# Reading the moving operand of every wide float32r product from two places in turn

## The chip, the cores and the metric

The kernel runs on one core of one Trainium2 chip. The metric is the device time of one execution in microseconds (us); lower is better. Engines are named as the profile names them: PE (the matmul array) with PEld (its weight loads), DVE, ACT, POOL, SP (which issues most DMAs).

## The reference

Two layers on 512 tokens of width 1024, all in float32. Each layer is a mixer and a SwiGLU feed-forward part, with norms, shifts, scales and gates that come from a conditioning vector.

```python
for layer in range(DEPTH):                       # DEPTH = 2
    mod = (cond @ ada_w[layer] + ada_b[layer])[:, None, :]
    sh1, sc1, g1, sh2, sc2, g2 = jnp.split(mod, 6, axis=-1)
    u = rms_norm(h, norm_g[layer, 0]) * (1.0 + sc1) + sh1
    y = hgrn2_mixer(...) if layer == 0 else dilated_attention_mixer(...)
    h = h + (1.0 + g1) * rms_norm(y, norm_g[layer, 1])
    u = rms_norm(h, norm_g[layer, 2]) * (1.0 + sc2) + sh2
    gate, up = jnp.split(u @ ffn_w_in, 2, axis=-1)
    y = (jax.nn.silu(gate) * up) @ ffn_w_out       # D_FF = 2816
    h = h + (1.0 + g2) * rms_norm(y, norm_g[layer, 3])
```

`hgrn2_mixer` projects u to queries, forget gates, values and output gates, and runs a chunked linear recurrence. `dilated_attention_mixer` projects u to queries, keys and values of three groups (dilations 1, 4, 16), applies rotary positions, and merges the groups' attention by their log-sums. Almost all arithmetic is in the dense projections.

## The kernel before, in words

**Products.** PE multiplies a stationary block of 128x128 by a moving block of 128 rows and up to 512 columns, into PSUM. To keep float32 accuracy, both factors are split into a high part (rounded to the type float32r) and a low rest: `oh`/`ol`, `hi`/`lo`, `uh`/`ul`, `th`/`tl`. ACT writes the high part by a copy with a cast, DVE the rest by a subtraction. Each product is three matmuls, high by high, high by low and low by high (helper `three`, L583 to L586; `run` at L965 and `products` at L1986 do the same). Each matmul has its own weight load. "Wide" is a float32r matmul with 256 or 512 moving columns.

**Stages, in order of time** (us from the start of the span):

- to 80: conditioning, and the token-major value product of layer 0 (`v_pass`, L1321: 8 weight rows x 3 parts x 8 banks = 192 matmuls of 512 columns).
- 80 to 280: the HGRN projections (`block`: 24 blocks x 24 = 576 matmuls of 512 columns), with the recurrence of eight heads (DVE mostly, and small matmuls) between them, and conditioning work of later parts.
- 280 to 360: the mixer's output product, the norm, and the first four column blocks of the feed-forward input (`mixer_out`, `half`, `block`).
- 360 to 525: the other 18 column blocks in `seven_products` (Strassen's scheme with seven half-size products: 84 matmuls of 256 columns a block; L965).
- 525 to 640: the feed-forward output (`prods` in `ffn`: 22 row blocks x 4 token blocks x 2 halves x 3 = 528 matmuls of 512 columns). Before each row block ACT and DVE split the middle activations (`part`: L580, L581) and the weights (L90, L91).
- 640 to 720: norms, the attention's value products (`v_prod`, `tok_proj`).
- 720 to 1140: attention. Here a planner (`Plan`) keeps a list of tasks with costs in us, due times and dependencies, tries several rules, and writes out the order for all engines. Its products are of three kinds: query and key blocks of group 0 (`plain`: 8 heads x 2 x 24 = 384 matmuls of 512 columns), of the other groups by seven products (`sevens`: 16 x 84 = 1344 of 256 columns), and values by seven products (`value_unit`: 4 x 7 x 24 = 672 of 256 columns).
- 1140 to 1487: output product, norm and feed-forward part of layer 1, as in layer 0.

In each of the two output products (mixers) there are 192 matmuls of 512 columns and then, in the first feed-forward blocks, 192 of 256 columns (`half`, L832, L835) and 96 of 512; `v_prod` and `tok_proj` have 96 of 512 each.

**Order.** In `mixer_out`, `seven_products`, the ends of `ffn` and the start, the order is written by hand (`manual_schedule`); elsewhere a scheduler of the framework orders the instructions; in attention `Plan` does.

**Places.** Tiles have offsets of 16 or 48 columns (`R0`, `V0`) and pads, so that operands stand at chosen addresses. `seven_products` and `products` also issue three extra matmuls ("asides") at the start of some runs of 256-wide products, with a moving operand shifted by 16 columns; their result is overwritten by the product that follows:

```python
if i == 0:
    for _ in range(3):
        pe.matmul(s.both, R[0][:, 0:P], uh[:, 0, 16:272], start=True, stop=True, ...)   # L992 to L994
```

The moving operand of a wide matmul is a row of neighbouring columns, its output a row of neighbouring columns of a PSUM bank.

Of the kernel before, what the change touches and what calls it, by code (L numbers as in the profile page):

```python
# [17 lines left out]
P = 128  # L18
# [16 lines left out]
WHOLE = ("quarters", "half")  # L35

# [104 lines left out]
class Plan:  # L141
# [5 lines left out]
    def __init__(self):  # L147
        self.tasks, self.names, self.seq, self.asides = [], {}, {}, set()
# [88 lines left out]
    def run(self):  # L237
# [15 lines left out]
        narrow = []  # L253
        for t in [t for t in done if t["eng"] == "PE"] + [{}]:
            if t.get("narrow"):
                narrow.append(t)
                continue
            first = next((k for k, u in enumerate(narrow) if u["aside"]), len(narrow))
            if len(narrow) - first >= 12:
                self.asides.add(narrow[first]["id"])  # L260
            narrow = []
# [40 lines left out]
def block_kernel(tc, x, c, positions, ada_w, ada_b, norm_g, hgrn_w_in, lower, hgrn_norm_g, hgrn_w_out,  # L302
# [8 lines left out]
    with ExitStack() as ctx:  # L311
# [271 lines left out]
        def three(ps, ah, al, bh, bl, start, stop, part=False):  # L583
            pe.matmul(ps, ah, bh, start=start, stop=False, skip_group_check=part)  # L584
            pe.matmul(ps, ah, bl, start=False, stop=False, skip_group_check=part)  # L585
            pe.matmul(ps, al, bh, start=False, stop=stop, skip_group_check=part)  # L586
# [18 lines left out]
        class Turn:  # L605
# [100 lines left out]
        def mixer_out(oT, otp, gate, l, side, close, made=None):  # L706
# [122 lines left out]
            for kt in range(KT):  # L829
                a = kt * 256  # L830
                for m, w in enumerate(fw[0]):
                    pe.matmul(pss[0][:, tok], w[:, a:a + P], uh[:, kt, tok], start=kt + m == 0, stop=False)  # L832
            for kt in range(KT):
                a = kt * 256
                pe.matmul(pss[0][:, tok], fw[0][0][:, a:a + P], ul[:, kt, tok], start=False, stop=kt == KT - 1)  # L835
# [53 lines left out]
        def seven_products(fs, mid, seeded, spare, th, tl):  # L889
# [71 lines left out]
            def run(ps, w, o, us, begin):  # L961
                for kt in range(4):
                    a = slice(o + kt * P, o + (kt + 1) * P)
                    for m, (x, y) in enumerate(((0, 0), (0, 1), (1, 0))):
                        pe.matmul(ps, w[x][:, a], us[kt][y], start=begin and kt + m == 0, stop=kt == 3 and m == 2,  # L965
# [10 lines left out]
            with tc.manual_schedule(engines=ORDERED):  # L976
# [10 lines left out]
                for i in range(len(fs)):  # L987
# [329 lines left out]
        def v_pass(e, which, hf, t):  # L1317
# [3 lines left out]
            pe.matmul(vbanks[hf, t], a, w, start=e == 0 and which == 0, stop=e == KT - 1 and which == 2)  # L1321
# [23 lines left out]
        with tc.manual_schedule(engines=ORDERED):  # L1345
# [121 lines left out]
            for (hf, t), b in vbanks.items():  # L1467
                (act.copy if hf == 0 else dve.tensor_copy)(v_tok[:, t, hf * 512:(hf + 1) * 512], b)
# [132 lines left out]
        def gate_pair(p):  # L1601
            whi, wlo = st.take()
            for k in range(2):
                ps = block(whi, wlo, k * P, 256)
                sg = fresh(qp, [P, S], "Q", 2)
                act.activation(sg, ps, AF.Sigmoid)
                dve.tensor_mul(sg, sg, ps)
# [917 lines left out]
```

## Time and profile before

| what | value |
|---|---|
| runs | 1492.56, 1493.22, 1494.55 us; median 1493.22 |
| span of the profiled execution | 1492.8 us, 25296 instructions |
| last matmul starts | 1486.3 us |
| PE busy | 1468.0 us (98%), 9915 matmul records |
| DVE, ACT, POOL busy | 74%, 54%, 13% |
| granted clock of PE | 0.999 of full speed, mean |

The profiled execution is known by its span: 1492.8 us, 0.4 us under the median of the runs. The "busy" time of a matmul is modelled and longer than its share of a stream (matmuls overlap), so the pace of a stream is read from the starts of neighbouring rows, not from durations. Durations on ACT and DVE are of one instruction. "x36" is a count; a line such as L585 can be that of a helper.

### The profile page before, as it was taken

Reading aid. Unit: us, or ns where it says so; the run is one execution under the profiler, and the core shown is the slowest. Engines: PE = TensorE matmul, PEld = TensorE weight load, DVE = VectorE, ACT = ScalarE, POOL = GpSimd, SP = SyncE. Lnnn points to the kernel's source line nnn. Section 1 sums busy time; section 2 is a strip of 40 time slices with the busy share of each in tenths; the row PEclk is TensorE's granted clock in tenths of the full one; section 3 lists DMA queues with packets and bytes.
Section 4 is the critical chain, followed back from the end, with each engine's and each line's share of the span. In section 5 each row is a group of like instructions: output and inputs, shape, how many; then the busy total and the mean of one; then the engine's idle time right before and its main releaser. Section 6 shows DMA issues by size and latency. Waiting matters only on the chain. (4 is left out here: it accounts for less than half of the span.)

```text
span 1492.8 us, 25296 instructions
## 1 busy us (share of the span) xinstructions
PE 1468.0 (98%) x9915; PEld 1318.0 (88%) x9915; DVE 1102.1 (74%) x1800; ACT 799.7 (54%) x1484; POOL 191.0 (13%) x173
## 2 busy tenths in 40 slices
PE   8999999999999999999999999999999999999998
PEld 6777788888999988778999999998988899999886
DVE  4578589488888875777798877888776978887533
ACT  4433433374555542257647878567885555555231
POOL 1011002030111100131001010001012211110100
PEclk9999999999999999999999999999999999999999
DMA  9556454213343346544334443354352333434531
GB/s 309 176 182 210 153 187 142 85 57 85 114 114 114 114 158 215 198 141 141 106 117 131 133 121 93 82 167 119 91 194 89 107 92 114 113 114 143 196 113 57
DMA packets 212872, 201.10 MB, mean 135 GB/s; under 512 B 8920, under 2 KB 170640, under 8 KB 212496
## 3 DMA queue, kind: packets, MB, share of 16 engines
q1 hardware_dynamic: 209776, 192.71, 41.6%
q10 hardware_dynamic: 1952, 6.65, 1.2%
q8 instruction: 78, 1.28, 0.4%
q0 software_dynamic: 1024, 0.12, 0.2%
q14 instruction: 42, 0.34, 0.1%
HBM read 192.30 MB, written 5.30 MB: 132 GB/s over the span
## 5 line engine op out<-in xcount | busy, mean ns | idle before, releaser
L90 ACT CAST hi<-raw 128x2048 fp32r<-128x2048 f32 x41 | 78.3, 1910 | 129.4 <-DMA raw<-in_ffn_w_out_dram 78.2
L1986 PE MATMUL ps_mm<-apart,hiq 128*128 128x256 f32 (+1 forms) x608 | 142.3, 326 | 0.8 <-ACT xs L2101 0.7
L91 DVE TENSOR_TENSOR lo<-raw,hi 128x2048 fp32r<-128x2048 f32 x41 | 97.9, 2391 | 57.8 <-ACT hi L90 57.7
L584 PE MATMUL ps_mm<-uh,hi 128*128 128x512 f32 (+1 forms) x368 | 133.8, 364 | 0.0
L585 PE MATMUL ps_mm<-ul,hi 128*128 128x512 f32 (+1 forms) x368 | 131.2, 356 | 1.1 <-DVE ul L684 1.1
L586 PE MATMUL ps_mm<-uh,lo 128*128 128x512 f32 (+1 forms) x368 | 131.3, 357 | 0.0
L1986 PEld LDWEIGHTS ps_mm<-apart,hiq 128*128 128x128 f32 x608 | 99.9, 189 | 9.4 <-ACT xs L2101 1.2
L956 DVE TENSOR_TENSOR loq<-raw,hiq 128x1024 fp32r<-128x1024 f32 x72 | 84.9, 1221 | 22.6 <-ACT hiq L952 22.6
L965 PE MATMUL ps_mm<-th,hiq 128*128 128x256 f32 x360 | 99.4, 276 | 0.0
L965 PE MATMUL ps_mm<-tl,hiq 128*128 128x256 f32 x360 | 99.4, 276 | 0.0
L965 PE MATMUL ps_mm<-th,loq 128*128 128x256 f32 x360 | 99.4, 276 | 0.0
L1986 PE MATMUL ps_mm<-apart,loq 128*128 128x256 f32 (+1 forms) x304 | 97.4, 320 | 0.5 <-DVE loq L2123 0.5
L936 POOL TENSOR_TENSOR raw<-raw 128x512 f32<-128x512 f32 x36 | 48.4, 1344 | 327.4 <-DVE spare L932 170.6
L585 PE MATMUL ps_mm<-lo,oh 128*128 128x512 f32 x208 | 81.6, 392 | 4.4 <-DVE lo L91 4.4
L584 PEld LDWEIGHTS ps_mm<-uh,hi 128*128 128x128 f32 x368 | 69.2, 188 | 15.4 <-issue 6.1
L952 ACT CAST hiq<-raw 128x1024 fp32r<-128x1024 f32 x72 | 72.1, 1047 | 19.4 <-DVE raw L940 16.1
L584 PE MATMUL ps_mm<-hi,oh 128*128 128x512 f32 x208 | 81.5, 393 | 0.1
L585 PEld LDWEIGHTS ps_mm<-ul,hi 128*128 128x128 f32 x368 | 69.3, 188 | 11.8 <-DVE ul L684 1.5
L586 PEld LDWEIGHTS ps_mm<-uh,lo 128*128 128x128 f32 x368 | 69.1, 188 | 10.4
L1986 PE MATMUL ps_mm<-uh,hiq 128*128 128x256 f32 x256 | 71.8, 281 | 0.0
L1986 PE MATMUL ps_mm<-ul,hiq 128*128 128x256 f32 x256 | 71.2, 278 | 0.0
L1986 PE MATMUL ps_mm<-uh,loq 128*128 128x256 f32 x256 | 71.2, 278 | 0.0
(484 smaller groups left out, 4688.6 us busy)
## 6 DMA issues: line engine op xcount, KB each, us to landing
raw<-in_ada_w_dram SPq DMA_DIRECT2D x40, 1024.0 KB, 5.2
raw<-in_ffn_w_in_dram SPq DMA_DIRECT2D x144, 256.0 KB, 4.1
raw<-in_ffn_w_out_dram SPq DMA_DIRECT2D x22, 1024.0 KB, 4.9
raw<-in_attn_w_in_dram SPq DMA_DIRECT2D x64, 256.0 KB, 4.2
raw<-in_hgrn_w_in_dram SPq DMA_DIRECT2D x12, 1024.0 KB, 5.4
raw<-in_attn_w_in_dram SPq DMA_DIRECT2D x12, 1024.0 KB, 5.3
raw<-in_ffn_w_in_dram SPq DMA_DIRECT2D x8, 1024.0 KB, 5.2
raw<-in_attn_w_in_dram SPq DMA_DIRECT2D x16, 512.0 KB, 5.3
```

Of the source, the lines that this page charges most:

```text
L90: self.nc.scalar.copy(hi, t)
L91: self.nc.vector.tensor_sub(lo, t, hi.bitcast(F32))
L584: pe.matmul(ps, ah, bh, start=start, stop=False, skip_group_check=part)
L585: pe.matmul(ps, ah, bl, start=False, stop=False, skip_group_check=part)
L586: pe.matmul(ps, al, bh, start=False, stop=stop, skip_group_check=part)
L936: pool.tensor_add(r[:, 2], r[:, 2], r[:, 0])
L952: act.copy(hi, src)
L956: dve.tensor_sub(lo, src, hi.bitcast(F32))
L965: pe.matmul(ps, w[x][:, a], us[kt][y], start=begin and kt + m == 0, stop=kt == 3 and m == 2, skip_group_check=True)
L1986: pe.matmul(dst(), x, y, start=begin and i == 0, stop=i == len(todo) - 1, skip_group_check=True)
```

## The change

Four views are added. `TAKE` reads a moving operand in blocks of 256 columns, and in each block column n and column n+128 in turn: 0, 128, 1, 129 and so on. `LAID` writes the output as before to neighbouring PSUM columns (it only has the same shape as `TAKE`). So output columns stand in the order in which they were read. `SEEN` reads such a row in the right order, with a step of two columns, and `PLACED` is the plain row that it is put in. All wide float32r products take `TAKE` and `LAID`.

The columns come back in order at the first reader that needs it: copies, gates, additions out of PSUM, or the split of `mid` in `part`. In `value_unit` the weights are instead split in such an order (`SEEN2`, `PLACED2` in `cut`) that the product comes out in order. Sums of squares and elementwise work between rows in the same order stay as they were.

The asides are gone with the code that placed them, and the planner's costs of products are other numbers. Eleven functions that nothing called (`qk_evac` to `pv_n`) are gone too.

```diff
+TAKE = lambda t: t.rearrange("p (x a n) -> p x n a", a=2, n=P)
+LAID = lambda t: t.rearrange("p (x n a) -> p x n a", a=2, n=P)
+SEEN = lambda t: t.rearrange("p (x n a) -> p x a n", a=2, n=P)
+PLACED = lambda t: t.rearrange("p (x a n) -> p x a n", a=2, n=P)
+SEEN2 = lambda t: t.rearrange("p s (n a) -> p s a n", a=2)
+PLACED2 = lambda t: t.rearrange("p s (a n) -> p s a n", a=2)
...
         def three(ps, ah, al, bh, bl, start, stop, part=False):
+            ps, bh, bl = LAID(ps), TAKE(bh), TAKE(bl)
             pe.matmul(ps, ah, bh, start=start, stop=False, skip_group_check=part)
...
-                dve.tensor_mul(self.yg[t, k], self.y[k][t], self.gate[:, k * 512:(k + 1) * 512])
+                dve.tensor_mul(PLACED(self.yg[t, k]), SEEN(self.y[k][t]), PLACED(self.gate[:, k * 512:(k + 1) * 512]))
...
-                        pe.matmul(ps, w[x][:, a], us[kt][y], start=begin and kt + m == 0, stop=kt == 3 and m == 2,
+                        pe.matmul(LAID(ps), w[x][:, a], TAKE(us[kt][y]), start=begin and kt + m == 0, stop=kt == 3 and m == 2,
...
-                    if i == 0:
-                        for _ in range(3):
-                            pe.matmul(s.both, R[0][:, 0:P], uh[:, 0, 16:272], start=True, stop=True, skip_group_check=True)
...
-                    split(oh, ol, mid(f))
+                    act.copy(PLACED(oh), SEEN(mid(f)))
+                    dve.tensor_sub(PLACED(ol), SEEN(mid(f)), PLACED(oh).bitcast(F32))
...
-                act.activation(T, ps, AF.Sigmoid)
+                act.activation(PLACED(T), SEEN(ps), AF.Sigmoid)
...
-                for _ in range(3 if me in plan.asides else 0):
-                    pe.matmul(dst(), todo[0][0], aside(), start=True, stop=True, skip_group_check=True)
                 for i, (x, y) in enumerate(todo):
-                    pe.matmul(dst(), x, y, start=begin and i == 0, stop=i == len(todo) - 1, skip_group_check=True)
+                    pe.matmul(LAID(dst()), x, TAKE(y), start=begin and i == 0, stop=i == len(todo) - 1, skip_group_check=True)
...
-                ACT(0.98, lambda: act.copy(G(p.t[0], o), C(raw.t, c)), [raw(c)], [p("h", o)])
-                DVE(1.17, lambda: dve.tensor_sub(G(p.t[1], o), C(raw.t, c), G(p.t[0], o).bitcast(F32)), [raw(c), p("h", o)], [p("l", o)])
+                ACT(0.98, lambda: act.copy(PLACED2(G(p.t[0], o)), SEEN2(C(raw.t, c))), [raw(c)], [p("h", o)])
+                DVE(1.17, lambda: dve.tensor_sub(PLACED2(G(p.t[1], o)), SEEN2(C(raw.t, c)), PLACED2(G(p.t[0], o)).bitcast(F32)), [raw(c), p("h", o)], [p("l", o)])
...
-            PE(0.68, go, [("oh", kt), ("ol", kt)] + [w(a, kt % 4 // 2) for a in "hl"], [b()])
+            PE(0.65, go, [("oh", kt), ("ol", kt)] + [w(a, kt % 4 // 2) for a in "hl"], [b()])
```

In order, PE has four rows fewer (twelve matmuls). SP's rows are the same, and outside attention ACT and DVE keep theirs. On PE at the start of `seven_products` in layer 0 (`spare`, `hiq`: split weights; `th`, `tl`: sums of `uh`, `ul`), before:

```order
L965 MATMUL ps_a_3246<-ul,spare_3103 128x256
L965 MATMUL ps_a_3246<-uh,spare_3104 128x256
L994 MATMUL ps_a_3248<-uh,spare_3103 128x256 x3
L965 MATMUL ps_a_3248<-th_3106,hiq_3252 128x256
L965 MATMUL ps_a_3248<-tl_3107,hiq_3252 128x256
```

and now:

```order
L963 MATMUL ps_a_3246<-ul,spare_3103 128x256
L963 MATMUL ps_a_3246<-uh,spare_3104 128x256
L963 MATMUL ps_a_3248<-th_3106,hiq_3252 128x256
L963 MATMUL ps_a_3248<-tl_3107,hiq_3252 128x256
```

The row with three asides is gone; the same happens in layer 1, and twice in attention (L1984). On ACT in attention, at the first value unit (`xs` and `qk`: copies out of PSUM; `hiq<-raw`: the split of weights in `cut`), before:

```order
L2018 COPY qk_6563<-shared 32x2x128
L2091 ACTIVATE shared<-ps_mm_6558 32x256
L2092 ACTIVATE qk_6568<-ps_mm_6558 128x256
L2101 COPY xs_6565<-ps_mm_6686 128x256
L2167 CAST hiq_6669<-raw_6655 128x1024
L2167 CAST hiq_6721<-raw_6655 128x1024
```

and now:

```order
L1853 COPY qk_6560<-shared 32x2x128
L2002 CAST hiq_6666<-raw_6652 128x1024
L1936 COPY xs_6562<-ps_mm_6684 128x256
L1926 ACTIVATE shared<-ps_mm_6555 32x256
L1927 ACTIVATE qk_6565<-ps_mm_6555 128x256
L2002 CAST hiq_6718<-raw_6652 128x1024
```

The first weight split now stands ahead of three copies out of PSUM instead of behind them. On PE late in attention the planner puts six 512-wide products ahead of the eight transposes (`ident`), before:

```order
L1986 MATMUL ps_mm_10381<-apart_6383,loq_10271 128x256
L2345 MATMUL ps_a_10451<-ident,h 128x128 x4
L2345 MATMUL ps_a_10487<-ident,h 128x128 x4
L1986 MATMUL ps_mm_10507<-apart_6383,hiq_10360 128x512
L1986 MATMUL ps_mm_10507<-apart_6384,hiq_10360 128x512
```

and now:

```order
L1822 MATMUL ps_mm_10389<-apart_6380,loq_10259 128x256
L1822 MATMUL ps_mm_10471<-apart_6380,hiq_10343 128x512
L1822 MATMUL ps_mm_10471<-apart_6381,hiq_10343 128x512
L1822 MATMUL ps_mm_10471<-apart_6380,loq_10344 128x512
L1822 MATMUL ps_mm_10471<-apart_6380,hiq_10343 128x512
L1822 MATMUL ps_mm_10471<-apart_6381,hiq_10343 128x512
L1822 MATMUL ps_mm_10471<-apart_6380,loq_10344 128x512
L2179 MATMUL ps_a_10372<-ident,h 128x128 x4
L2179 MATMUL ps_a_10453<-ident,h 128x128 x4
```

Such shifts by a few rows are all that the planner's new costs do.

More of the change, by code (lines that the diff above doesn't have):

```diff
@@ L147, in __init__ @@
     def __init__(self):
-        self.tasks, self.names, self.seq, self.asides = [], {}, {}, set()
+        self.tasks, self.names, self.seq = [], {}, {}
     def add(self, eng, cost, fn=None, r=(), w=(), goal=None, late=None, urgent=False):
@@ L252, in run @@
             t["start"], t["due"] = start[t["id"]], due[t["id"]]
[L253 to L261, printed above, removed]
         for t in done:
@@ L1320, in v_pass @@
             w = (vlo if which == 2 else vhi)[e // 2][:, e % 2, hf * 512:(hf + 1) * 512]
-            pe.matmul(vbanks[hf, t], a, w, start=e == 0 and which == 0, stop=e == KT - 1 and which == 2)
+            pe.matmul(LAID(vbanks[hf, t]), a, TAKE(w), start=e == 0 and which == 0, stop=e == KT - 1 and which == 2)
         lbt = sp.tile([P, 3, 8], F32, name="lbt")
@@ L1868, in pv_n @@
-        def pv_n(hd):
-            st_ = heads.pop(hd)
-            hs = slice((hd % 4) * P, (hd % 4 + 1) * P)
-            b = bank("b")
-            for t in range(NT):
-                sl = slice(t * P, (t + 1) * P)
-                pe.matmul(b[:, sl], V[0][:, t, hs], st_["pn"][:, sl], start=True, stop=t == 0)
-                if t:
-                    pe.matmul(b[:, sl], V[0][:, t - 1, hs], st_["p0"][:, sl], start=False, stop=True)
-            dve.tensor_add(oT[hd], oT[hd], b)
         plan = Plan()
@@ L2069, in terms @@
                         yield triple(p.t[0][:, w], p.t[1][:, w], *us[kt])
-                products(12 * 0.1137, lambda: b.t[:, lo], b(), terms, begin, [p("h", part), p("l", part)])
+                products(12 * 0.1116, lambda: b.t[:, lo], b(), terms, begin, [p("h", part), p("l", part)])
             def products_1():
```

175 lines of the change are left out of this document (19 added, 156 removed).

## The prediction

> **What bounds the kernel now.** I read the page first, then stretches of the span by engine, then the chain of work and the order of time on PE for its pace.
>
> ```profile
> span 1492.8 us, 25296 instructions
> PE 1468.0 (98%) x9915; PEld 1318.0 (88%) x9915; DVE 1102.1 (74%) x1800; ACT 799.7 (54%) x1484; POOL 191.0 (13%) x173
> ...
> PEclk9999999999999999999999999999999999999999
> ```
>
> PE is nearly always busy at full clock. The question is therefore how fast a stream of matmuls runs, and where PE has company. The stretches (span, then busy us of PE, PEld, DVE, ACT, POOL with counts, granted clock, DMA share, GB/s):
>
> ```profile
> 360.00:525.00 165.00, 165.00 (x1440) 164.32 (x1438) 130.91 (x135) 91.65 (x151) 21.98 (x17) 1.00 0.38 109
> 1186.00:1370.00 184.00, 184.00 (x1570) 181.86 (x1569) 145.04 (x153) 102.25 (x166) 21.98 (x17) 1.00 0.37 110
> 525.00:640.00 115.00, 111.68 (x533) 93.61 (x532) 76.65 (x118) 34.84 (x41) 15.56 (x6) 0.99 0.58 197
> 1370.00:1486.00 116.00, 116.00 (x513) 96.04 (x513) 57.52 (x62) 32.03 (x42) 8.43 (x5) 1.00 0.37 130
> 80.00:280.00 200.00, 198.71 (x1220) 159.85 (x1219) 156.68 (x291) 75.99 (x161) 29.72 (x24) 1.00 0.50 165
> 720.00:1100.00 380.00, 376.50 (x2885) 359.06 (x2884) 307.13 (x684) 274.18 (x592) 30.29 (x33) 1.00 0.41 119
> 20.00:80.00 60.00, 59.39 (x351) 43.07 (x350) 29.68 (x62) 25.64 (x34) 1.51 (x3) 1.00 0.78 231
> ```
>
> In the first four (seven products and the feed-forward output, twice) PE works without a break, but for 3.3 us in the third, and DVE has 20% or more to spare. In the HGRN stage DVE is at 78% and PE's matmuls hang on its recurrence; in attention DVE is at 81% and ACT at 72%. The first value product stands beside the densest loads (DMA share 0.78).
>
> The pace of 256-wide products, from the chain of work (start, us, what), and of 512-wide ones, from the order of time on PE:
>
> ```profile
> 1201.09 4.08 PE ps_mm L965 x36
> 1205.17 2.72 PE ps_b L965 x24
> ```
>
> ```profile
> 1439.63 0.39 PE L584 MATMUL ps_b<-hi,oh 128*128 128x512 f32 x1
> ...
> 1441.67 0.39 PE L584 MATMUL ps_mm<-hi,oh 128*128 128x512 f32 x1
> ```
>
> 4.08/36 and 2.72/24 give 113.3 ns for 256 columns. Of the 512-wide, nine start from 1439.63 until 1441.67 (2.04 us, three trios of 0.68): 226.7 ns. Both are 0.4427 ns per column, with nothing left over per instruction. One place shows what the array could do. After a stall PE runs at half clock for two microseconds (first the order of time, then the stretch with its granted clock):
>
> ```profile
> 605.87 0.63 PE L584 MATMUL ps_a<-hi,oh 128*128 128x512 f32 x1
> 606.30 0.63 PE L585 MATMUL ps_a<-lo,oh 128*128 128x512 f32 x1
> 606.72 0.63 PE L586 MATMUL ps_a<-hi,ol 128*128 128x512 f32 x1
> 607.15 0.63 PE L584 MATMUL ps_mm<-hi,oh 128*128 128x512 f32 x1
> ```
>
> ```profile
> 605.40:607.40 2.00, 2.00 (x6) 1.57 (x5) 2.00 (x9) 0.00 (x0) 0.00 (x0) 0.50 0.62 154
> ```
>
> 1.28 us for three starts: 426.7 ns at a clock of 0.50. Twice that clock would give 213.3 ns, but the same products take 226.7 = 213.3 x 17/16. So at full clock one column's time in 16 (64 bytes of a row of float32) is lost, and at half clock none. A loss that goes away when columns are taken at half the pace belongs to the supply of the moving columns, not to the array. That is what the change touches.
>
> **The change, part by part.**
>
> *512-wide products.* Floor 213.3 ns; if the loss stays, 226.7; if each column of the new order pays, far more (second rival). In the new order each of the two places is read at half the pace, which is the condition of the half-clock rows, and these are without loss. I take 216, just over the floor, since no row at full clock comes down to it: 10.7 ns less each. The counts follow from the loops: 1056 in the feed-forward output, 576 in HGRN projections, 192 in the first value product, 384 in attention, and 768 elsewhere (two output products of 192, two feed-forward blocks of 96, 96 each in `v_prod` and `tok_proj`): 2976.
>
> The Trainium skill ("TensorE: Matmul & The Clock Gate", section "Wait — 56ns, not 53.3ns?") has N/2.4 + 2.5 ns for warm matmuls in a stream and N/1.2 for cold ones, whatever order the columns are read in. The half-clock rows agree with the second (427), the stream does not agree with the first (227 against 216). By the rule alone nothing would be lost now, and the change would be worth the asides only, 1.4 us; as 227 is measured, the trace decides.
>
> *256-wide products.* The same floor would be 107 ns, but each has a weight load. Matmuls of one column show what a load costs by itself:
>
> ```profile
> 231.61 1.02 PE L430 MATMUL ps_b<-ones,shared 128*128 128x1 f32 x8 [0.30 <-DVE T L1504]
> 232.50 0.48 PE L584 MATMUL ps_mm<-uh,hi 128*128 128x512 f32 x1
> ```
>
> 0.89/8 = 0.111 us. So 111.5 instead of 113.3 ns, 1.8 less. In attention some streams run slower:
>
> ```profile
> 773.43 0.28 PE L1986 MATMUL ps_mm<-uh,loq 128*128 128x256 f32 x1
> 773.55 0.28 PE L1986 MATMUL ps_mm<-uh,hiq 128*128 128x256 f32 x1
> ...
> 773.91 0.28 PE L1986 MATMUL ps_mm<-uh,hiq 128*128 128x256 f32 x1
> ```
>
> 0.12 each (0.48 for four). Between 1.8 (all as in seven products) and 7 (all at 118.5), I take 3.4 for attention, about a third in the slow form. Counts: 3024 in seven products (2 layers x 18 x 84), 2016 in attention, 384 in `half`: 5424.
>
> *Asides.* 12 matmuls x 0.113 = 1.4 us less, half of it in seven products.
>
> *Readers out of order.* ACT and DVE take as many instructions as before. What a step costs:
>
> ```profile
> L2146 ACT ACTIVATE qk<-ps_mm 128x512 f32<-128x512 f32 x16 | 9.5, 594 | 21.4 <-PE ps_mm L1986 21.4
> L2353 ACT COPY h<-ps_a 128x512 f32<-128x512 f32 x24 | 13.5, 592 | 1.0 <-PE ps_a L2345 0.8
> L580 ACT CAST oh<-mid 128x512 fp32r<-128x512 f32 x44 | 26.2, 618 | 57.6 <-PE ps_b L585 44.4 <-PE ps_mm L585 10.4 <-DVE a L861 1.4
> L1704 ACT CAST apart<-uh 128x512 fp32r<-128x512 f32 x8 | 8.3, 1126 | 0.2 <-POOL ul L684 0.2
> L1705 DVE CAST apart<-ul 128x512 fp32r<-128x512 f32 x8 | 4.3, 624 | 0.0
> L581 DVE TENSOR_TENSOR ol<-mid,oh 128x512 fp32r<-128x512 f32 x44 | 29.7, 685 | 18.7 <-ACT oh L580 18.7
> L2167 ACT CAST hiq<-raw 128x1024 fp32r<-128x1024 f32 x28 | 28.9, 1049 | 22.9 <-DVE raw L2172 11.0 <-DMA raw<-in_attn_w_in_dram 10.7 <-PE ps_a L1986 0.8
> ```
>
> L2146 already reads PSUM in steps of 128 columns and takes no longer than L2353: nothing for ACT's readers of PSUM. L1705 reads SBUF on DVE in steps of four columns and stays under the plain L581: nothing for DVE either; for its reads of PSUM, where no row has a step, I take the same, with up to its 0.69 again as the other end. L1704, ACT reading SBUF in steps of four columns, takes 1126 against 618. The new step is two columns, at 44 casts (L580) and 28 (L2167): between nothing and +0.51 and +1.02 us each, 22 and 29 us of ACT. The first lies beside the feed-forward output, where ACT is busy under a third, and costs nothing there; the second would bring ACT in attention from 274 to 303 of 380 us and might cost PE a third of it, 10 us. I take nothing, and keep +10 for the range.
>
> The Trainium skill ("SBUF — State Buffer", section "Specifications (TRN2)") has lines of 16 bytes that need two hits each for full bandwidth: a step of two float32 columns has them, one of four has not, and L1704 agrees. For these casts the sum by the rule is the same.
>
> *Order.* SP's rows are the same, so no transfer changes its turn. In attention the first weight split stands ahead of three copies out of PSUM; behind them waits the next accumulation, for about the 1.05 us of the split. PE's transposes stand behind six products. I count each as nothing: PE has other products queued in those places, and a microsecond either way is inside the range.
>
> *The sum.* Full, and what I keep of it:
> - feed-forward output 1056 x 10.7 = 11.3, kept, PE being alone on the path
> - seven products 3024 x 1.8 = 5.4 and asides 0.7, kept
> - output products, feed-forward blocks, `v_prod`, `tok_proj`: 768 x 10.7 = 8.2, and `half` 384 x 3 = 1.2 (some of them slow as above); the norms between them wait on ACT and DVE, so 8.0 kept
> - attention 384 x 10.7 = 4.1, 2016 x 3.4 = 6.9, asides 0.7: 11.7, kept 7.7, as DVE is late next
> - HGRN 576 x 10.7 = 6.2, kept 3.8; there the recurrence on DVE is late next
> - first value product 192 x 10.7 = 2.1, kept 1.0, as the loads of that stretch don't get faster.
>
> Together 46.8, kept 37.9. 1492.8 - 37.9 = 1454.9 for the profiled execution, whose span is 0.4 us under the median of the runs (1493.2); I say 1455.
>
> **Rivals.**
>
> *Other engines take the gain.* For it: DVE's 307 of 380 us and 157 of 200. Then only the first four stretches gain, 17.4, and a quarter of the remaining 29: 24.7 us, 1468. Against it: even there PE has few breaks. 0.13.
>
> *Slower: each column of the new order pays.* Neighbours in time are now 512 bytes apart, and no matmul of this trace reads so. For it: L1704, where a step past 16 bytes doubles an engine's reading. If PE falls to a column every second cycle, as in the half-clock rows (427 instead of 227 ns, and 213 instead of 113), the loss is 2976 x 0.2 + 5424 x 0.1 = 1138 us: 2631. The products have 2.91 million columns; against the 46.8 us to be had, 0.016 ns more per column decides. Against it: L2146 and L1705 step as far or over the same 16 bytes and lose nothing. 0.09, for any amount over 0.2%.
>
> The Trainium skill's rule on lines, named above, speaks for this rival: taken in turn, each column comes from another line, with one hit a visit. No run so far shows it for PE.
>
> *It does nothing.* The lost cycle may belong to the 64 bytes themselves: each place still crosses one every 16 of its own columns, and 17/16 stays. Then 1492.8 - 1.4 is 1491.4. Without the asides the 256-wide streams of seven products could even fall to 118.5: 3024 x 5.2 = 16 us more, 1507, which belongs to the slower cases. 0.04 for no change.
>
> **How the numbers follow.** My forecast has 0.74, between 1438 (all 46.8 kept, and attention's slow streams all mended, 7 instead of 3.4, another 7) and 1465 (ACT's 10 us). Other engines taking the gain 0.13, up to 1482. Slower 0.09, nothing 0.04. From 1438 to 1480 leaves out the slower and the unchanged case and a little of the others. Within 0.2% (3 us), about what a measurement of this kernel can tell from no change, only "nothing" falls. Faster 0.87, same 0.04, slower 0.09.
>
> **What would show it.** Right: starts in the feed-forward output 0.216 apart and trios of 0.65; seven products at 4.0 for 36; L580's successor still near 618 ns, L2167's near 1049; no 118 in attention. Wrong: starts at 0.227 (nothing), over 0.23 (slower), or PE faster but with new waits on DVE's and ACT's splits in attention, HGRN and the norms (gain taken). A doubled ACT cast would show in attention as PE waiting for `hiq`.

## The result and the profile after

The changed kernel takes 1476.65 us (median; 1474.33 to 1478.71) beside 1492.89 us (1489.05 to 1494.55) of the kernel before on the same chip: a ratio of 0.9893, 95% interval 0.9875 to 0.991. It is 16 us faster, where 38 had been forecast; the time lies inside the range, near its upper end. (Of all executions in this text one, of experiment e5, took 5236.67 us beside 1467 to 1474 for its others; e5's ratio leaves it out, and without it e5's median would be 1470.4.) The profiled execution has these lines at the head of its page:

```profile
span 1474.1 us, 25335 instructions
PE 1430.7 (97%) x9903; PEld 1312.5 (89%) x9903; DVE 1113.8 (76%) x1800; ACT 824.7 (56%) x1484; POOL 190.1 (13%) x173
```

PE is busy 37 us less, yet the span is only 18.7 us shorter; and DVE and ACT, with no instruction more, are busy 12 and 25 us longer. The rest of this text follows from these two facts. First PE's pace, from the order of time on PE in the feed-forward output and from the chain of work in the seven products:

```profile
1425.07 0.38 PE L582 MATMUL ps_mm<-hi,oh 128*128 128x512 f32 x1
...
1427.01 0.38 PE L582 MATMUL ps_a<-hi,oh 128*128 128x512 f32 x1
```

```profile
1209.26 4.02 PE ps_mm L963 x36
```

Nine starts in 1.94 us are 215.6 ns, and 4.02/36 is 111.7 ns: the two prices of the forecast (216 and 111.5). The stretches of the span show where this gain didn't arrive (span, then busy us of PE, PEld, DVE, ACT, POOL, granted clock, DMA share, GB/s); after, and then the two of before that correspond to the first and second:

```profile
524.00:650.00 126.00, 119.74 (x543) 102.19 (x542) 91.75 (x140) 48.53 (x63) 20.94 (x11) 0.97 0.56 186
650.00:702.00 52.00, 46.19 (x213) 39.47 (x212) 39.40 (x55) 36.44 (x54) 11.58 (x15) 0.97 0.37 122
702.00:1082.00 380.00, 368.97 (x2853) 353.67 (x2852) 309.71 (x665) 282.35 (x573) 29.61 (x31) 1.00 0.40 117
```

```profile
536.00:664.00 128.00, 123.43 (x544) 101.33 (x543) 90.11 (x142) 43.49 (x62) 20.98 (x11) 0.99 0.54 182
664.00:710.00 46.00, 45.33 (x209) 37.44 (x208) 35.00 (x51) 32.70 (x53) 11.66 (x15) 1.00 0.41 138
```

The feed-forward output of layer 0 (first row) has 6 us without PE, where before it had 4.6, and a lower granted clock; the products of `v_prod` and `tok_proj` (second row) take 52 instead of 46 us; attention (third) is as long as before, 380 us. The list of stages given with the kernel before is rough: in the trace of before the seven products of layer 0 end at 535.5 us and its feed-forward output at 663.9. Set out by stage, from the first and last wide product of each in the two traces:

| stage | before, us | after, us | gained | forecast |
|---|---|---|---|---|
| to the end of the first value product | 75.4 | 73.2 | 2.2 | 1.0 |
| HGRN, output product and blocks of layer 0 | 277.4 | 271.4 | 6.0 | 6.9 |
| seven products, both layers | 365.8 | 358.8 | 7.0 | 6.1 |
| feed-forward output, layer 0 | 128.4 | 126.6 | 1.8 | 5.6 |
| `v_prod`, `tok_proj` | 46.1 | 51.2 | -5.1 | 1.8 |
| attention | 380.3 | 380.7 | -0.4 | 7.7 |
| output product and blocks of layer 1 | 93.6 | 92.3 | 1.3 | 3.1 |
| feed-forward output, layer 1 | 119.7 | 114.0 | 5.7 | 5.6 |

(The forecast's 3.8 for HGRN and 8.0 for four kinds of product are shared out by their counts.) Three rows hold what is missing between these two executions: 3.8, 6.9 and 8.1 us make 18.8 of 19.2. Each column is one execution, and a stage varies by 2 us or so: in e4 below, whose code outside attention is that of the changed kernel, the feed-forward output of layer 0 takes 128.9 us. PE's longest waits for other engines in the whole trace (us in total, times, longest) lie there:

```profile
PE ps_mm L583 <- DVE lo L97: 5.4, 4, 3.3
PE ps_mm L582 <- ACT hi L96: 4.2, 3, 3.4
PE ps_mm L1822 <- DVE loq L2003: 4.0, 5, 0.9
```

Before, the corresponding list has this row, 0.5 us for `loq`, and none for `hi`:

```profile
PE ps_mm L585 <- DVE lo L91: 4.4, 2, 3.2
```

And the groups of instructions (busy us, mean ns of one) show casts that have grown:

```profile
L2002 ACT CAST hiq<-raw 128x1024 fp32r<-128x1024 f32 x28 | 37.1, 1350 | 18.0 <-DVE raw L2007 7.9 <-DMA raw<-in_attn_w_in_dram 7.3 <-PE ps_mm L1822 2.5
L1063 ACT CAST oh<-mid 128x512 fp32r<-128x512 f32 x44 | 36.5, 855 | 35.8 <-PE ps_b L583 27.1 <-PE ps_mm L583 7.4 <-PE ps_mm L963 1.2
L1064 DVE TENSOR_TENSOR ol<-mid,oh 128x512 fp32r<-128x512 f32 x44 | 36.0, 828 | 13.1 <-ACT oh L1063 13.1
L1700 ACT CAST apart<-uh 128x512 fp32r<-128x512 f32 x8 | 11.7, 1547 | 0.2 <-POOL ul L682 0.2
L1701 DVE CAST apart<-ul 128x512 fp32r<-128x512 f32 x8 | 6.6, 988 | 0.0
```

L2002, L1063 and L1064 have the change's step of two columns: 1049, 618 and 685 ns have become 1350, 855 and 828. But L1700 and L1701, `apart`, are word for word the code of before, and have gone from 1126 to 1547 and from 624 to 988 ns. The last of the eight `apart` on ACT starts at 680.5 us, when PE stands still, and takes 1084 ns; the other seven take 1526 to 1659. So it is not only that a step has its price.

A second loss lies across the stages. PE runs at half clock in five stretches of 3.4 or 6.8 us (from 15, 227, 592, 684 and 1022 us), each in or behind a pause of 1.5 to 3.4 us, and before in one (from 604 us). The stretch at 227 lies in HGRN:

```profile
226.80:230.20 3.40, 3.40 (x14) 3.02 (x14) 3.33 (x6) 0.69 (x1) 1.91 (x1) 0.50 0.22 80
```

PE is busy for 18.7 us of these five stretches, and for 3.0 of the one before. Half of that time, 9.3 and 1.5 us, is an estimate of what they cost: some 8 of the 19.2 us that are missing, more than half of it inside the three rows named above.

### The profile page after: what moved, and what is told of

Same layout as the page of the kernel before. It is cut to its first block, busy times and chain, and to the rows that moved or that the text cites. A ratio compares the mean times of both kernels' runs of the same rounds, so it can differ in the third digit from the quotient of the medians.

```text
span 1474.1 us, 25335 instructions
## 1 busy us (share of the span) xinstructions
PE 1430.7 (97%) x9903; PEld 1312.5 (89%) x9903; DVE 1113.8 (76%) x1800; ACT 824.7 (56%) x1484; POOL 190.1 (13%) x173
## 5 line engine op out<-in xcount | busy, mean ns | idle before, releaser
L1822 PE MATMUL ps_mm<-apart,hiq 128*128 128x256 f32 (+1 forms) x608 | 137.4, 320 | 3.5 <-ACT xs L1936 2.8
L582 PE MATMUL ps_mm<-uh,hi 128*128 128x512 f32 (+1 forms) x368 | 130.7, 355 | 0.0
L583 PE MATMUL ps_mm<-ul,hi 128*128 128x512 f32 (+1 forms) x368 | 128.4, 349 | 1.6 <-DVE ul L682 1.6
L584 PE MATMUL ps_mm<-uh,lo 128*128 128x512 f32 (+1 forms) x368 | 128.3, 349 | 0.0
L950 ACT CAST hiq<-raw 128x1024 fp32r<-128x1024 f32 x72 | 72.2, 1049 | 21.1 <-DVE raw L938 16.5
```

Source lines behind the costliest of these rows:

```text
L950: act.copy(hi, src)
L1822: pe.matmul(LAID(dst()), x, TAKE(y), start=begin and i == 0, stop=i == len(todo) - 1, skip_group_check=True)
```

## The experiments

Three theories for the missing 20 us: the step itself ("steps"); TensorE's new way of reading, which slows the other engines' strided reading beside it ("contention"); and a PE that now runs into limits which nothing has moved, above all the ring of two raw weight tiles, the buffers in which weights land before they are split ("supply").

**e1: TensorE's reading alone.** All readers of the changed kernel go back to plain order:

```
-SEEN = lambda t: t.rearrange("p (x n a) -> p x a n", a=2, n=P)
+SEEN = lambda t: t            # PLACED, SEEN2, PLACED2 alike
```

> The changed kernel with TensorE's reading as it is (two places in turn, 215.8 and 111.7 ns), but every reader of PSUM and every weight cast in the plain order of before: no step of two columns is left on ScalarE or VectorE, and the columns of the result stay out of order. Theory 'steps' (the 22 us that are missing against the forecast went into casts with a step and the waits behind them): the two stretches that lost, feed-forward output of layer 0 and attention, get back most of it; 1460 to 1466, oh<-mid at 618 ns again. Theory 'supply' (the weight ring, VectorE and the norms cannot go faster, however the casts read): within 4 us of the changed kernel, 1473 to 1479, with the same waits of PE for the splits. Theory 'contention' (TensorE reading two places slows every strided access to SBUF): apart<-uh, whose code is the same in all versions, stays near 1550 instead of 1126 ns, with the wait of 3.5 us behind it.

Measured: 1470.78 us, ratio 0.986 (0.9844 to 0.9877). By the ratios some 5 us come back, less than "steps" asked for and more than "supply". Attention takes 374.8 instead of 380.7 us, the feed-forward output of layer 0 stays at 127.1. And `apart`, with every step of the change gone from the kernel, stays slow:

```profile
L1700 ACT CAST apart<-uh 128x512 fp32r<-128x512 f32 x8 | 11.6, 1571 | 0.2 <-POOL ul L682 0.2
```

**e2: the steps alone**, in the kernel before (TensorE reads as it did):

```
-                    split(oh, ol, mid(f))
+                    act.copy(PLACED(oh), SEEN(mid(f)))
+                    dve.tensor_sub(PLACED(ol), SEEN(mid(f)), PLACED(oh).bitcast(F32))
```

> The kernel before, with the step of two columns put into the casts of oh, ol and of the value weights alone; TensorE reads as before (226.7 and 113.4 ns). The columns of these operands are out of order, so the result is not the reference's. If the step itself is what costs: oh<-mid near 855 ns and ol<-mid,oh near 828 as in the changed kernel. If only TensorE's new reading makes it dear ('contention'): under 700 and under 720. The time: 'steps' some 3 to 10 us over before (1496 to 1503), as PE is slower here and leaves the casts more time; 'supply' within 2 us of before.

Measured: 1492.24 us, ratio 1.001 (1.0002 to 1.0019): 1.5 us slower. The same casts with the same step, without TensorE's new reading beside them:

```profile
L2173 ACT CAST hiq<-raw 128x1024 fp32r<-128x1024 f32 x28 | 31.5, 1146 | 20.9 <-DVE raw L2178 11.2 <-DMA raw<-in_attn_w_in_dram 9.1 <-PE ps_a L1992 0.3
L1074 DVE TENSOR_TENSOR ol<-mid,oh 128x512 fp32r<-128x512 f32 x44 | 29.7, 685 | 19.5 <-ACT oh L1073 19.5
L1073 ACT CAST oh<-mid 128x512 fp32r<-128x512 f32 x44 | 28.1, 658 | 60.6 <-PE ps_b L590 49.2 <-PE ps_mm L590 9.9 <-PE ps_mm L970 1.4
```

A step of two costs ACT 40 ns on 618 and 97 on 1049, and DVE nothing. The other 197 and 204 ns on ACT, and all 143 on DVE, are there only together with TensorE's new reading.

**e3: pairs.** Two neighbouring columns from each place in turn, each pair put back in its place in PSUM, no reader changed:

```
+TAKE = lambda t: t.rearrange("p (a n b) -> p n a b", a=2, b=2)   # and LAID the same
```

> TensorE takes two neighbouring columns from each of two places in turn (256 columns apart in 512-wide products, 128 in 256-wide) and writes each pair back to its own place in PSUM, so that the result is in order and no reader or cast has a step. If the loss of one column in 16 goes away whenever two places take turns: 216 and 111.7 ns, and the time of e1 (1460 to 1466 by 'steps', 1473 to 1479 by 'supply'). If it goes away only when every column changes place, or if PSUM written in pieces of two columns costs: 220 to 227 ns or more, and 1480 to 1495.

Measured: 2081.22 us, ratio 1.395 (1.3932 to 1.3968). A miss on both of its branches. Three starts of 512 columns and a chain entry of 24 of 256 columns:

```profile
1990.23 0.50 PE L582 MATMUL ps_b<-hi,oh 128*128 128x512 f32 x1
...
1991.22 0.50 PE L582 MATMUL ps_mm<-hi,oh 128*128 128x512 f32 x1
```

```profile
488.43 3.95 PE ps_a L963 x24
```

330 and 164.6 ns, half as much again as 215.8 and 111.7. So "two places in turn" isn't enough to describe what helps; and the rival of a cost in every column was nearer than it looked.

**e4: the planner's old costs**, in attention alone:

```
-                products(12 * 0.1116, lambda: b.t[:, lo], ...
+                products(12 * 0.1137, lambda: b.t[:, lo], ...
...
-                        products(6 * 0.2159, lambda: b.t, ...
+                        products(6 * 0.2275, lambda: b.t, ...
...
-            PE(0.65, go, ...
+            PE(0.68, go, ...
```

> The changed kernel with the planner's three costs of products of before (0.1137, 0.1165 and 0.2275 us per matmul and 0.68 per trio), so attention is planned as if PE were slow. If the waits that are new in attention come from the new order: attention 3 to 8 us shorter, 1469 to 1474. If they come from casts or from PE's pace: within 3 us of the changed kernel, 1474 to 1480, or a little over.

Measured: 1472.38 us, ratio 0.9878 (0.9857 to 0.9899). Its interval overlaps that of the changed kernel; attention is 378.4 us. Whether the order adds a little or nothing is not told apart.

**e5: the steps moved to PSUM.** Gates, sums and value products read PSUM out of order; the casts out of SBUF are plain:

```
-                act.copy(W[:, 6 + i % 2], s.u4)
+                act.copy(PLACED(W[:, 6 + i % 2]), SEEN(s.u4))
-                    act.copy(PLACED(oh), SEEN(mid(f)))
+                    split(oh, ol, mid(f))          # and so on for W, xs, the value sums
```

> The changed kernel with every step of two columns moved to where ScalarE and VectorE read PSUM (the gates and sums of the seven products, the sums of the value products, the copies of xs); oh, ol and the value weights are cast in plain order, and the columns of the result are in order. 'Steps in SBUF under TensorE's new reading': PSUM reads with a step stay at their plain duration, oh<-mid at 618, the value casts at 1047 ns, and the time is that of TensorE alone, 1467 to 1474. 'A step costs wherever it is read': the seven products' readers of PSUM slow down, and the time stays at 1474 to 1480.

Measured: 1470.85 us, ratio 0.9862 (0.9837 to 0.9887), the time of e1. The sum of the seven products takes 415 ns with the step (415 without, in the changed kernel), and the cast is plain again:

```profile
L971 DVE TENSOR_TENSOR shared<-shared,ps_mm 128x256 f32<-128x256 f32 x36 | 14.9, 415 | 0.5 <-PE ps_mm L963 0.5
L577 ACT CAST oh<-mid 128x512 fp32r<-128x512 f32 x44 | 25.9, 616 | 43.7 <-PE ps_b L583 32.9 <-PE ps_mm L583 9.5 <-PE ps_mm L963 1.3
```

So a step is free where PSUM is read, as the prediction had it, and taking it away from the reads of SBUF was worth 5 us.

**e6: fed.** Weights split in halves, and `apart` written behind the weight casts of `tok_proj`:

```
-                self.nc.scalar.copy(hi, t)
-                self.nc.vector.tensor_sub(lo, t, hi.bitcast(F32))
+                for c in (slice(0, 1024), slice(1024, 2048)):
+                    self.nc.scalar.copy(hi[:, c], t[:, c])
+                    self.nc.vector.tensor_sub(lo[:, c], t[:, c], hi[:, c].bitcast(F32))
...
             ws = [st.take(), st.take(1)]
+            between()          # the eight casts of apart
```

> The changed kernel with two edits to what PE waits for, none to what it computes: each streamed weight is split in two halves (cast, difference, cast, difference) so that PE can start on the first, and the eight casts of apart stand behind the casts of the weights of tok_proj instead of ahead of them. 'Supply' (PE now outruns the ring of two raw tiles and its splits): pauses of PE in the feed-forward output of layer 0 fall from 11 to 3 to 6 us, the 3.5 us at 680 go, and with them two to four of the stretches at half clock of 3.4 us: 1460 to 1468. 'Steps' (the slow casts alone hold PE up): the wait at 680 goes but the feed-forward output keeps over 9 us: 1470 to 1474.

Measured: 1468.99 us, ratio 0.9855 (0.9837 to 0.9873), between the two ranges that had been expected. The feed-forward output of layer 0 falls from 126.6 to 122.4 us, and to 120.1 and 119.6 in the other versions with halves (e7, e11); without them it takes 124.2 to 128.9. So supply was real there. The ring in the changed kernel shows how (order of time, of transfers and splits):

```profile
579.16 0.38 SPq L76 DMA_DIRECT2D raw<-in_ada_w_dram  x1
579.76 0.38 SPq L76 DMA_DIRECT2D raw<-in_ffn_w_out_dram  x1
...
587.99 1.90 ACT L96 CAST hi<-raw 128x2048 fp32r<-128x2048 f32 x1 [8.37 <-DMA raw<-in_ffn_w_out_dram]
...
589.92 3.78 DVE L97 TENSOR_TENSOR lo<-raw,hi 128x2048 fp32r<-128x2048 f32 x1 [0.70 <-ACT hi L96]
593.73 0.37 SPq L76 DMA_DIRECT2D raw<-in_ffn_w_out_dram  x1
```

From one issue to the next of the same raw tile are 13.97 us: 8.2 until the weights have landed behind a tile of the conditioning, 1.9 for the cast, 3.8 for the difference (the longest of ten; their median is 2.3). PE uses up such a tile (48 products) in 48 x 0.2158 = 10.4 us; before, in 10.9. It stands still here for 3.3 us (the longest wait for `lo` above), until the difference is done, and then runs at half clock until 598.8:

```profile
595.40:598.80 3.40, 3.40 (x10) 2.67 (x9) 2.37 (x9) 0.24 (x1) 0.00 (x0) 0.50 0.80 297
```

This longest turn is not new. Before, it took 14.24 us, and PE waited 3.2 us for `lo`:

```profile
590.58 0.38 SPq L70 DMA_DIRECT2D raw<-in_ffn_w_out_dram  x1
604.82 0.37 SPq L70 DMA_DIRECT2D raw<-in_ffn_w_out_dram  x1
```

What is new is that the stage's pauses add up to 6.3 us instead of 4.6, with a stretch of 6.8 instead of 3.4 us at half clock behind the longest. No run puts the halves into the kernel before, so how much of their gain belongs to this change is not shown.

The second edit missed. The wait at 675 us stayed at 3.0, since `apart` kept its place ahead of the cast: the weights are issued at 668.2, and ACT was free for `apart` at 666.0 and busy with it for 11.4 us.

**e7: both**, the edits of e5 and of e6.

> Both of the edits above in one kernel. If the two causes are separate and add up: 1454 to 1462, about the forecast, with PE's pauses from 540 to 700 us under 6 us and the mean granted clock at 0.996 or more. If one hides the other, or attention and HGRN keep the rest: 1462 to 1470.

Measured: 1465.52 us, ratio 0.9828 (0.9804 to 0.9853). By the ratios the gains add up (0.0031 and 0.0038, together 0.0065), but the time is that of the second branch: the forecast isn't reached, and the wait for `hi` behind `apart` (1572 ns) is still 3.0 us.

**e8: other orders of reading**, one execution: 16 and 64 apart in the feed-forward output of layers 0 and 1, a step of two and 4 apart in the seven products of layers 0 and 1, pairs in the first value product, plain order in `v_prod` and `tok_proj`:

```
+    "16": (lambda t: t.rearrange("p (x a n) -> p x n a", a=2, n=16), ...
+    "64": (lambda t: t.rearrange("p (x a n) -> p x n a", a=2, n=64), ...
+    "4": (lambda t: t.rearrange("p (x a n) -> p x n a", a=2, n=4), ...
+    "step2": (lambda t: t.rearrange("p (n a) -> p a n", a=2), ...
+    "pairs": (lambda t: t.rearrange("p (a n b) -> p n a b", a=2, b=2), ...
```

> One look at the pace of PE and at who slows down beside it; columns end out of order. Two places in turn 16 columns apart in the feed-forward output of layer 0, 64 apart in that of layer 1; a step of two columns in the seven products of layer 0, two places 4 columns apart in those of layer 1; pairs of columns from two places, written in one piece, in the first value product; v_prod and tok_proj read in plain order. If the loss belongs to columns that follow each other inside 64 bytes: 16 and 64 apart run at 215.8, 4 apart (always in the same or next 64 bytes) and the step of two at 113.3 or more. If every second access to another place is enough: 4 apart at 111.7 as well. The pairs at 330 of e3 come from reading if they stay near 330 here, from PSUM written in pieces if they come to 227 or less. 'Contention': with v_prod in plain order, apart<-uh is back at 1126 ns; if it stays near 1550, TensorE's reading isn't the cause.

PE's starts: seven products of layer 0 (a step of two), of layer 1 (4 apart), and the feed-forward output of layer 0 (16 apart):

```profile
499.99 0.42 PE L973 MATMUL ps_mm<-th,loq 128*128 128x256 f32 x1
500.22 0.43 PE L973 MATMUL ps_mm<-th,hiq 128*128 128x256 f32 x1
```

```profile
1419.92 0.28 PE L973 MATMUL ps_mm<-th,hiq 128*128 128x256 f32 x1
1420.03 0.28 PE L973 MATMUL ps_mm<-tl,hiq 128*128 128x256 f32 x1
```

```profile
740.04 0.38 PE L590 MATMUL ps_mm<-hi,oh 128*128 128x512 f32 x1
...
740.69 0.38 PE L590 MATMUL ps_a<-hi,oh 128*128 128x512 f32 x1
```

230 ns for 256 columns with a step of two, twice the plain 113.3; 111.7 at 4 columns apart; 215.8 at 16 (and at 64) apart. The pairs of the first value product, written in one piece, run at 333 ns: it is the reading of pairs that costs, not the writing. The surprise is beside PE. First `apart` next to a `v_prod` in plain order, then `oh` next to products 16 apart (layer 0), and 64 apart (layer 1):

```profile
L1713 ACT CAST apart<-uh 128x512 fp32r<-128x512 f32 x8 | 8.3, 1155 | 0.2 <-POOL ul L690 0.2
```

```profile
L1076 ACT CAST oh<-mid 128x512 fp32r<-128x512 f32 x21 | 13.4, 664 | 20.0 <-PE ps_b L591 12.0 <-PE ps_mm L591 6.0 <-PE ps_mm L973 2.0
```

```profile
L1076 ACT CAST oh<-mid 128x512 fp32r<-128x512 f32 x22 | 18.4, 863 | 25.0 <-PE ps_b L591 20.6 <-PE ps_mm L591 3.8 <-PE ps_mm L973 0.6
```

Contention is shown (1155 for 1547 when only TensorE's order beside it changes), and it depends on the distance: at 16 columns apart PE has the full pace, and the casts take 664 ns, where the step alone costs 658.

**e9: 16 columns apart**, steps and readers as in the changed kernel; the plain heads and value products of attention stay at 128:

```
-TAKE = lambda t: t.rearrange("p (x a n) -> p x n a", a=2, n=P)
+TAKE = lambda t: t.rearrange("p (x a n) -> p x n a", a=2, n=16)    # LAID, SEEN, PLACED too
```

> The changed kernel with the two places 16 columns apart instead of 128, in all wide products but those of the plain heads and the value weights in attention (768 by 512 wide at most stay as they were); the readers put blocks of 16 back in order, with the same steps of two columns as in the changed kernel. 'Contention belongs to the distance' (from the one look: oh<-mid 663 at 16 columns, 862 at 64): oh<-mid near 660, ol<-mid,oh near 684, apart<-uh near 1140, PE at 215.8 and 111.7 as before; with the casts short again the time comes to that of e1 and e5, 1466 to 1472. If the pauses are supply's alone: 1473 to 1478. If runs of 16 columns cost the readers of PSUM more than runs of 128: their rows get longer, and attention with them, over 1478.

Measured: 1465.12 us, ratio 0.983 (0.9816 to 0.9844), 9 us better than the changed kernel, with one number of the code changed.

```profile
L1067 ACT CAST oh<-mid 128x512 fp32r<-128x512 f32 x44 | 28.6, 673 | 44.0 <-PE ps_b L587 32.6 <-PE ps_mm L587 8.9 <-DVE shared L404 1.3
L1704 ACT CAST apart<-uh 128x512 fp32r<-128x512 f32 x8 | 8.6, 1198 | 0.2 <-POOL ul L686 0.2
```

And the stretch of `v_prod` and `tok_proj`:

```profile
648.00:694.00 46.00, 43.69 (x209) 37.58 (x208) 36.05 (x53) 32.48 (x53) 11.58 (x15) 1.00 0.41 138
```

That stage is back from 51.2 to 46.0 us with 0.2 us of wait for `hi` in all; attention takes 377.0.

**e10: e9 and e5 together**, the steps at PSUM and the distance at 16.

> e9 with the steps moved to the readers of PSUM as in e5, so neither a step nor contention is left on the casts outside attention. 'Contention': a little under e5 (1470.85), as apart and the HGRN stage's strided rows are also back: 1465 to 1470. 'Supply': the same as e5 within 3 us, with 9 us or more of pauses left in the feed-forward output of layer 0.

Measured: 1463.52 us, ratio 0.9814 (0.9801 to 0.9827). That is 7 us under e5, more than "supply" allowed. Attention takes 372.0 us; its value casts have no step left. The feed-forward output of layer 0 stays at 127.9; that this is supply is shown by e11.

**e11: e10 and e6 together**, halves of weights added.

> e10 with the weights split in halves and apart behind the casts as in e6: every cause found so far taken away at once. If steps, contention and supply are all there is besides attention's and HGRN's own limits: 1457 to 1464, and the wait of 3.2 us at 675 under 1.5, since apart is done 3 us sooner. If the half clock after the pauses in HGRN and attention keeps its share: 1463 to 1467, as e7.

Measured: 1457.86 us (1457.22 to 1459.47), ratio 0.9784 (0.9771 to 0.9798): the fastest version, 32 us under before. The feed-forward output of layer 0, and PE's longest waits:

```profile
523.00:643.00 120.00, 116.97 (x548) 101.78 (x548) 92.66 (x154) 44.38 (x74) 21.88 (x11) 1.00 0.59 195
```

```profile
PE ps_b L668 <- DVE xn L662: 3.4, 4, 1.1
PE ps_a L2130 <- ACT h L2193: 2.9, 2, 2.0
PE ps_mm L587 <- ACT oh L582: 2.6, 2, 1.3
```

No wait for a weight split is among them. Attention is 374.1, `v_prod` and `tok_proj` 45.5, the feed-forward output of layer 0 119.6 us.

**e12: where contention begins**, one execution, e9 with 32 columns apart in the feed-forward output of layer 0, 8 in that of layer 1, 4 in `v_prod`:

```
+WAY = lambda n: (lambda t: t.rearrange("p (x a n) -> p x n a", a=2, n=n), ...
+    ..., f == NF - 1, way=WAY(32 if l == 0 else 8))
+    ..., kt == KT - 1, way=WAY(4))
```

> One look at where the contention begins, on e9: the two places stand 32 columns (128 bytes) apart in the feed-forward output of layer 0, 8 apart (32 bytes) in that of layer 1, and 4 apart (16 bytes) in v_prod; the columns of these products end out of order. PE's pace should stay at 215.8 ns in all three. Known so far for the casts beside it: 16 apart 663 to 673 ns (oh<-mid), 64 and 128 apart 855 to 865. If the border is a fixed distance between 64 and 256 bytes, 8 apart is at 660 and 32 apart is either; if contention grows with distance, 32 apart lies between, at 700 to 800. apart<-uh beside v_prod at 4 apart: 1130 to 1200 if nearness is what helps, near 1550 if any other order than the plain one disturbs it.

Layer 0, then layer 1:

```profile
L1068 ACT CAST oh<-mid 128x512 fp32r<-128x512 f32 x21 | 13.8, 678 | 12.3 <-PE ps_b L588 7.8 <-PE ps_mm L588 4.5
```

```profile
L1068 ACT CAST oh<-mid 128x512 fp32r<-128x512 f32 x22 | 14.1, 668 | 30.8 <-PE ps_b L588 25.7 <-PE ps_mm L588 4.5 <-PE ps_mm L968 0.6
```

678 at 32 and 668 at 8 apart; `apart` is at 1135 beside a `v_prod` at 4 apart; PE at 215.8 in all three. So 4 to 32 columns leave the others alone, and 64 and 128 do not: for these casts the border lies between 128 and 256 bytes. Why the distance decides, no run shows.

## Why the prediction was wrong, step by step

*The pace: right; the reason for it: only in part.* 216 and 111.5 ns were taken, 215.8 and 111.7 came, in attention too, where no product is left at 118. That the order of reading alone changes the pace bears out that the loss belongs to the supply of the moving columns. The reason why this order should help (each place is read at half the pace) does not tell it from pairs, which also read each place at half the pace and take 330 ns; so the choice of a good order was partly luck. The seven products gained 7.0 (6.1 forecast, the asides among them), layer 1's feed-forward output 5.7 (5.6), HGRN with its neighbours 6.0 (6.9).

*"I take nothing" for readers out of order: the step that failed.* It priced each reader by a row in which TensorE read in plain order. ACT's casts of 618 and 1049 ns came to 855 and 1350, inside the two ends that had been set (up to 0.51 and 1.02 us more); DVE's difference, held at nothing because L1705 "stays under the plain L581", came to 828 for 685. By e2 the step alone is a sixth of the first and a third of the second, and nothing on DVE; the rest is contention, which the prediction had no term for, and which reached instructions that the change doesn't touch. Going from 128 to 16 columns (e9) alone returns 9 us, and moving the steps to PSUM (e5) alone 5; both (e10) 12 of the 22 that were missing.

*A term that was not there: what a pause costs behind it.* The prediction's own rows show half clock after a stall, but its sum has no term for it. In the profiled execution some 9 us were lost so, against 1.5 before (an estimate, worked out above). In the other versions it is between 4.8 (e9) and 11.3 (e7).

*"Lies beside the feed-forward output, where ACT is busy under a third, and costs nothing there": not contradicted.* With plain casts that stage takes 127.1, 125.3 and 127.9 us (e1, e5, e10), with stepped ones 126.6 and 128.9 (after, e4): no difference beyond that between executions. The price was paid elsewhere. In `tok_proj` ACT worked through `apart` for 11.7 instead of 8.3 us, and the next weight cast stood behind it: 3.4 us of wait, and 3.4 us at half clock after it. In attention the loss is what the prediction kept as "+10 for the range": with plain casts it takes 372 to 376 us (e1, e5, e7, e10, e11), with stepped casts at 128 columns 378 to 381 (after, e4, e6), and 377.0 and 374.9 in e9 and e12, where of the casts only those of the value weights are slow (one execution each).

*"Feed-forward output ... 11.3, kept, PE being alone on the path": wrong for layer 0.* The row shown had 3.3 us of pause, and that "DVE has 20% or more to spare" was read as room. That row ends at 640 us; over the whole stage, to 663.9, PE already lacked 4.6 us. The limit was no engine's busy time but the loop of a raw tile: transfer, cast, difference, next issue. PE's faster use met it (10.4 us per tile against a loop of up to 14), so 1.8 of 5.6 came. Halving the splits (e6) gave 4.2 us back, and in e11 the stage is 119.6: the pauses of before are gone too.

*The rival "other engines take the gain", at 0.13 and 1468 us*, was the nearest to what happened, with another mechanism than the one that it named: not that DVE was full, but that ACT and DVE were made slower by PE.

*"Slower: each column of the new order pays"* fell for this order, with 215.8 ns. But e3 and e8 show how near it lay: pairs cost 330 ns per 512 columns, a step of two 230 per 256. The Trainium skill's rule on lines of 16 bytes ("SBUF — State Buffer", section "Specifications (TRN2)"), which spoke for this rival, doesn't sort these: at 128 columns apart every visit to a line has one hit and nothing is lost, while a step of two, with two hits in a row, takes twice as long.

*Order* was costed at nothing. e4 leaves that open: 1472.38 us, with an interval that holds the changed kernel's ratio.

*What stays open:* by its ratio e11 gains 32 us where 38 had been forecast, and part of that comes from pauses that the kernel before had as well. The half-clock stretches after pauses come and go between executions (mean granted clock 0.990 to 0.998 in these versions, 0.995 to 1.000 in the kernel before), and what they cost in each stage was not measured apart.

## What to carry to other kernels

Price an instruction from a row in which its neighbours on the other engines do what they will do after the change: a new access pattern on TensorE is a change to ACT and DVE too. When the busiest engine gets faster, look for the loop that feeds it (issue, landing, split, next issue) and set its length beside what the engine then uses up; spare busy time says nothing about it. Count a pause with the half-clock stretch that may follow it. And if a reading order has a free parameter such as the distance, try a few values, and read the other engines' rows as well as the one that was meant to gain.

## What the runs showed of the hardware

Reading order of a float32r moving operand, ns per 512 columns at full clock: in plain order 226.7; two places in turn, 16, 64 or 128 columns apart, 215.8 (and 4 and 8 apart, 111.7 per 256 and 215.8); pairs from two places 330; a step of two columns 230 per 256.

Strided reading of SBUF by ACT and DVE slows while TensorE reads two places 128 columns apart: `apart` on ACT from 1126 to 1547 and on DVE from 624 to 988 ns, a step of two on ACT from 658 to 855 and on DVE from 685 to 828. At 64 columns apart the step of two on ACT takes 863. Plain casts beside the same products don't (617, e1), nor do reads of PSUM (415, e5). With 4 to 32 columns between the places these rows stay near what they are beside plain reading: 664 to 678 ns for the step of two on ACT, 1135 to 1198 for `apart`. The Trainium skill ("SBUF — State Buffer", section "SBUF: two separate sides") says that PE, ACT and DVE's own ports never wait on anyone; these rows differ, and the measurement decides.

A pause of PE of 1.5 to 3.4 us was often, not always, followed by 3.4 or 6.8 us at a granted clock of 0.50. By estimate, with half of PE's busy time in such a stretch taken as lost, a wait of 3.3 us cost 5 to 6.
